# A hybrid decoder step on one core: the later adaLN columns made four pairs at a time

## The chip, the core and the metric

One Trainium2 chip, one of its NeuronCores. The metric is the time of one execution of the program on the device, in microseconds (us). The median of three runs of the kernel before is 998.04 us (995.92 to 1000.73).

## What is computed

One inference step of one decoder layer for 512 prompt tokens and 8 samples of 8 tokens (576 columns in all, width 1024). What matters here is the modulation, which every norm and every residual uses:

```python
cs = silu(c)                                   # 1 prompt row + 8 sample rows, width 1024
mod = cs @ ada_w + ada_b                       # (9, 6144)
sh1, sc1, g1, sh2, sc2, g2 = split(mod, 6)
h = rmsnorm(x, norm1_w) * (1 + sc1) + sh1
x = x + g1 * mixer(h)                          # in-projection, SSD | mLSTM | RG-LRU, out-projection
h = rmsnorm(x, norm2_w) * (1 + sc2) + sh2
x = x + g2 * (square(relu(h @ mlp_up)) @ mlp_down)
y = rmsnorm(x, final_norm_w)
```

`ada_w` has 1024 x 6144 weights of 4 bytes, 25 MB, for nine rows of `c`.

## The kernel before

Activations lie with the 1024 features on partitions, eight tiles (K tiles) of 128, and tokens along the free axis. A weight block of 128 output features is a tile `raw` of 128 x 1024, loaded by SP (line 128, three buffers), and split by ACT (`wh`, line 150) and DVE or GpSimd (`wl`, line 152) into two parts; `mm_k` (line 164) makes three products of it for each K tile and each half of the tokens, into an accumulator `g` of two PSUM banks. A block has 48 of these matmuls. In this text they are called block matmuls. There are 124 blocks: the in-projection, 16 of the out-projection, then the MLP.

Beside the blocks run generators: the SSD step of each head group and chunk (`ssd`), the mLSTM of each head (`mlstm`), the RG-LRU, the norms, and `ada_gen`. `unit` (line 179) calls `slot` in the middle and at the end of each block; a slot lets every active generator go on to its next `yield`. So a `yield` says after how many half blocks the next piece is written. The instructions are then put into queues by a list scheduler with a cost model of its own, which takes program order as priority and gives out tiles from pools: the final order on each engine is the scheduler's, and each engine works its queue off strictly in that order. SP's queue is also the order of nearly all loads.

Small products take PSUM tiles from the pool `psm` by `P()` (line 96): four tiles of one bank each, for all generators. In an SSD step `cb` and `xt` are two such tiles, `py` and `ps` two more: `cb` holds B C and B turned, `xt` the tokens of x turned (line 691); DVE makes `xdt` and `xend` from `xt` (line 698) and `att` from `cumb` (line 707), and TensorE makes `py` and `ps` from them (lines 729 to 734). In an mLSTM, `num` becomes `pt` by transposes (line 1063), and `pi` is C times q (line 1003).

The 6144 columns of `mod` are made in 24 pairs of 128 columns; pair q ends up in `modt[:, q]` (128 features x 2 x 9 rows). The first eight pairs (shift and scale of the first norm) are made at the start of the kernel and stay as they are. The pairs 8 to 23 are `ada_gen`'s, active from the second element of `ORDER` on. For each pair it loads two slabs of 128 x 1024 (line 238, 512 KB each, two buffers), waits `ADA_WAIT` = 3 slots, and then calls `ada_mm`: eight matmuls with `cs` of one K tile (32 columns, nine of them used) as weights and 256 columns of the slab as moving data. K tile k goes to column group k % 4 of the array, so that four K tiles run side by side and the bank `adap` holds four partial sums on its partitions 32j to 32j + 31. ACT copies the bank to `adarow` (line 220). A slot later `ada_sel` multiplies each half of `adarow` with the 0/1 matrix `sel` (line 228), which adds up the four partial sums and turns them onto partitions, and DVE adds the bias (line 229). After one more slot the next pair begins.

Of the kernel before, what the change touches and what calls it, by code (L numbers as in the profile page):

```python
# [22 lines left out]
FT = mybir.dt.float32  # L23
FR = mybir.dt.float32r
BF = mybir.dt.bfloat16
AF = mybir.ActivationFunctionType
OP = mybir.AluOpType
# [10 lines left out]
D, KT = 1024, 8  # L38
# [29 lines left out]
class Kernel:  # L68
# [162 lines left out]
                                op=OP.add)  # L231

    def ada_gen(self):
        for q in range(8, 24):
            t = []
            for c in range(2):
                t.append(self.rpool.tile([128, 1024], FT, name=self.name("ada"), tag="ada", bufs=2))
                self.nc.sync.dma_start(t[c], self.io["ada"][q, :, c * 1024:(c + 1) * 1024])
                if q == 8:
                    self.after(self.start_dma)  # L240
            for _ in range(ADA_WAIT):
                yield
            row = self.ada_mm(lambda k: t[k // 4][:, (k % 4) * 256:(k % 4 + 1) * 256])
            yield
            self.ada_sel(q, row)
            self.done.add(f"ada{q}")
            for _ in range(ADA_REST):
                yield

# [1212 lines left out]


N_TILES = 54
ADA_WAIT, ADA_REST = 3, 1
WARM = 14, 4, 4, 6
PAIR_AT = 3
W_AT = {0: 1, 2: 2, 4: 3}  # L1470
# [33 lines left out]
def _layout(a):  # L1504
    f = np.float32
    out = {}
    x = np.concatenate([a["x_prompt"].reshape(TP, D), a["x_sample"].reshape(TS, D)])
    out["x"] = x.T.reshape(KT, 128, NT).transpose(1, 0, 2)
    c = np.zeros((32, D), f)
# [3 lines left out]
    chunks = [v * 8 + k for pair in ((0, 1), (2, 3)) for k in range(8) for v in pair]  # L1513
    chunks += [4 * 8 + k for k in range(8)] + [5 * 8 + k for k in range(8)]
    w = a["ada_w"][0].reshape(KT, 128, 48, 128)[:, :, chunks]
    out["ada"] = w.reshape(KT, 128, 24, 2, 128).transpose(2, 1, 0, 3, 4).reshape(24, 128, 2048)
    ab = a["ada_b"][0].reshape(48, 128)[chunks].T

    w_in = a["w_in"][0]
# [1 line left out]
    z, xbc, dt, q, k, v, o, ig, fg, xr, gr = (w_in[:, pts[i]:pts[i + 1]] for i in range(11))  # L1521
# [50 lines left out]
    i = np.arange(128)  # L1572
# [3 lines left out]
    j = np.arange(64)  # L1576
# [5 lines left out]
    row = np.concatenate([np.arange(16), np.arange(32, 36), np.arange(64, 68)])  # L1582
# [56 lines left out]
```

## Time and profile before

| what | value |
|---|---|
| median of three runs (lowest, highest) | 998.04 us (995.92, 1000.73) |
| the profiled execution's own time | 995.4 us |
| its span, first to last instruction | 993.6 us |
| TensorE busy (share of the span) | 959.5 us (97%) |
| VectorE (DVE), ScalarE (ACT), GpSimd (POOL) busy | 590.2, 399.8, 203.8 us |
| mean granted clock of TensorE | 0.987 |
| moved by DMA | 119.62 MB, 120 GB/s |

The profile is of one execution. A row of the timeline has the start and the length in us, the engine, the line of the kernel, the operation, out<-in and a count; in brackets stands how long the engine was idle before and what ended that. PE is TensorE's matmuls, PEld its weight loads; a plain fp32 matmul leaves two records of each, one a pass. The ends of matmuls are modelled and overlap, so costs are read from starts. The time beyond the span, 1.8 us, is what lies around the program's instructions.

### The profile page before, as it was taken

The numbers are of one execution on the slowest core, as the hardware profiler recorded it, in microseconds if no ns is written. First come the engines' busy times: TensorE is split into PE (matmuls) and PEld (weight loads), VectorE is DVE, ScalarE is ACT, GpSimd is POOL, SyncE is SP. The second block draws the span as 40 slices with busy tenths as digits, with TensorE's granted clock in tenths as the row PEclk, the third lists the DMA queues.
The fourth block names the chain that finished last, engine by engine and source line by source line (L and its number), as shares of the span: only waits on it lengthen the run. The fifth ranks groups of instructions, "written<-read, shape, count | busy, mean of one in ns | idle before, by whom it ended". The sixth has DMA issues, their size and how long they took to land.

```text
span 993.6 us, 18146 instructions
## 1 busy us (share of the span) xinstructions
PE 959.5 (97%) x7369; PEld 904.1 (91%) x7370; DVE 590.2 (59%) x1180; ACT 399.8 (40%) x741; POOL 203.8 (21%) x220
## 2 busy tenths in 40 slices
PE   8999789889999999999999999999999999999996
PEld 5889778777788899999999999999999999999996
DVE  4669897887788377468444455533553355335544
ACT  3454744453646674345222234312441144114320
POOL 2836454532355532020000000000000000000032
PEclk8999999998999999999999999999999999999998
DMA  9721254654464333444222322222222222222202
GB/s 343 294 86 64 81 186 133 246 173 137 131 223 153 105 137 129 140 131 162 91 98 105 110 86 84 74 79 84 85 86 85 86 85 76 76 83 85 85 23 96
DMA packets 51220, 119.62 MB, mean 120 GB/s; under 512 B 6956, under 2 KB 17468, under 8 KB 51136
## 3 DMA queue, kind: packets, MB, share of 16 engines
q1 hardware_dynamic: 47024, 111.06, 32.7%
q10 hardware_dynamic: 3744, 6.85, 1.8%
q8 instruction: 58, 0.95, 0.4%
q0 software_dynamic: 368, 0.55, 0.2%
q14 instruction: 26, 0.21, 0.1%
HBM read 108.68 MB, written 9.76 MB: 119 GB/s over the span
## 4 chain that ended last, share of the span: by engine, by line
PE 76%; DVE 10%; ACT 4%; issue 3%; DMA 1%; POOL 0%; POOLq 0%; DVEq 0%; ACTq 0%
PE g L164 66%; DVE r L626 3%; PE adap L218 1%; PE g L1363 1%; DMA nmb<-scr_nm 1%; PE py L729 1%; PE lg L1129 1%; DVE att L707 1%; PE ps L734 1%; PE py L732 1%; DVE nmb L924 1%; DVE xbc L651 0%; DVE sp_e L494 0%; PE adas L228 0%; ACT r L620 0%
## 5 line engine op out<-in xcount | busy, mean ns | idle before, releaser
L150 ACT ACTIVATE wh<-raw 128x1024 fp32r<-128x1024 f32 x123 | 130.1, 1058 | 333.9 <-PE g L164 309.4
L164 PE MATMUL g<-hnh,wh 128*128 128x288 f32 x688 | 153.1, 302 | 10.1 <-ACT r L614 8.0
L164 PE MATMUL g<-hnh,wl 128*128 128x288 f32 x688 | 152.1, 299 | 0.6 <-DVE wl L152 0.6
L164 PE MATMUL g<-hnl,wh 128*128 128x288 f32 x688 | 151.8, 299 | 0.0
L152 DVE TENSOR_TENSOR wl<-raw,wh 128x1024 fp32r<-128x1024 f32 x97 | 118.7, 1225 | 29.5 <-ACT wh L150 29.4
L164 PEld LDWEIGHTS g<-hnh,wh 128*128 128x128 f32 x688 | 110.4, 189 | 19.3 <-ACT r L614 9.2
L164 PEld LDWEIGHTS g<-hnh,wl 128*128 128x128 f32 x688 | 111.6, 189 | 2.7 <-issue 1.2
L164 PEld LDWEIGHTS g<-hnl,wh 128*128 128x128 f32 x688 | 111.7, 189 | 0.8 <-issue 0.4
L164 PE MATMUL g<-h2h,wh 128*128 128x288 f32 (+1 forms) x512 | 110.9, 297 | 0.0
L164 PE MATMUL g<-h2l,wh 128*128 128x288 f32 (+1 forms) x512 | 110.9, 298 | 0.0
L164 PE MATMUL g<-h2h,wl 128*128 128x288 f32 (+1 forms) x512 | 110.0, 296 | 0.0
L307 DVE SCALAR_TENSOR_TENSOR xr<-g,modt,xr 128x288 f32<-128x288 f32 x38 | 19.7, 518 | 141.2 <-PE g L164 141.2
L164 PE MATMUL g<-hh,wl 128*128 128x288 f32 x480 | 102.9, 295 | 0.0
L164 PE MATMUL g<-hh,wh 128*128 128x288 f32 x480 | 102.5, 295 | 0.0
L164 PE MATMUL g<-hl,wh 128*128 128x288 f32 x480 | 102.4, 295 | 0.0
L1405 POOL TENSOR_SCALAR xr<-xr,vec 128x576 f32<-128x576 f32 (+2 forms) x8 | 15.2, 1900 | 383.8 <-ACT sqa L1237 363.4
L152 POOL TENSOR_TENSOR wl<-raw,wh 128x1024 fp32r<-128x1024 f32 x26 | 69.0, 2653 | 80.3 <-ACT wh L150 61.4
L164 PEld LDWEIGHTS g<-h2h,wl 128*128 128x128 f32 x512 | 83.4, 188 | 0.0
L164 PEld LDWEIGHTS g<-h2h,wh 128*128 128x128 f32 x512 | 83.1, 189 | 0.1
L164 PEld LDWEIGHTS g<-h2l,wh 128*128 128x128 f32 x512 | 83.0, 188 | 0.0
L164 PEld LDWEIGHTS g<-hh,wh 128*128 128x128 f32 x480 | 77.0, 188 | 0.0
L164 PEld LDWEIGHTS g<-hh,wl 128*128 128x128 f32 x480 | 77.0, 188 | 0.0
(399 smaller groups left out, 1652.7 us busy)
## 6 DMA issues: line engine op xcount, KB each, us to landing
raw<-w SPq DMA_DIRECT2D x124, 512.0 KB, 3.5
ada<-ada SPq DMA_DIRECT2D x32, 512.0 KB, 5.6
ada<-ada SPq DMA_DIRECT2D x32, 256.0 KB, 5.9
cumb<-scr_cum SPq DMA_DIRECT2D x16, 256.0 KB, 5.6
s<-s SPq DMA_DIRECT2D x16, 256.0 KB, 4.7
ssm_s<-s ACTq DMA_DIRECT2D x16, 256.0 KB, 2.9
x<-x SPq DMA_DIRECT2D x8, 288.0 KB, 4.7
xr<-x SPq DMA_DIRECT2D x8, 288.0 KB, 3.9
```

Source lines behind the costliest of these rows:

```text
L150: nc.scalar.activation(hi, raw, AF.Copy)
L152: eng.tensor_tensor(lo, raw, hi.bitcast(FT), op=OP.subtract)
L164: self.nc.tensor.matmul(pg.h[h][:m, :e], w(k), xx[:, h * HALF:h * HALF + e], start=start and n == 0, stop=stop and n == 2)
L218: nc.tensor.matmul(ps[32 * j:32 * j + 32, :256], self.cs[:, k, :], ks(k), start=k < 4, stop=k >= 4)
L307: self.nc.vector.scalar_tensor_tensor(dst[:, :HALF], pg.h[0][:, :HALF], gate[:, 0:1], x[:, :HALF], op0=OP.mult, op1=OP.add)
L626: nc.vector.scalar_tensor_tensor(a[:, :n], r[:, j:j + n], wcols[:, j:j + 1], a[:, :n], op0=OP.mult, op1=OP.add)
L707: self.eng("att").tensor_scalar(E[:, h * 128:(h + 1) * 128], cums[h2][:, h * 128:(h + 1) * 128], self.col1[:, c, hd:hd + 1], 0.0, op0=OP.a ...
L729: nc.tensor.matmul(o, xdt[:, h * 64:(h + 1) * 64], att[h // 4][:, hs], start=True, stop=not c)
L732: nc.tensor.matmul(o, S[:, h * 64:(h + 1) * 64], ce[h // 4][:, hs], start=False, stop=True)
L734: nc.tensor.matmul(pst, cb[:, 128:256], xend[:, :512], start=True, stop=True)
L924: self.eng("nmb").tensor_scalar(E[:, tk(c)], nmb[:, tk(c)], ecol(c), 0.0, op0=OP.add, op1=OP.min)
L1405: self.eng("fin").tensor_scalar(x, x, self.v("fnw")[:, o:o + 1], None, op0=OP.mult)
```

## The change

The 16 later pairs are made in four groups of four. The weights lie in DRAM in another order (`ada4`): slab i of a group holds K tile k of all four pairs, 4 x 256 columns. For each slab four matmuls run, all with the same weights `cs[:, k]`: pair j of the group goes to column group j, and its sum over all eight K tiles is made in PSUM. So `adap` is taken at the first slab of a group and given back after ACT's copy at the last. The partitions 32j to 32j + 31 of `adarow` then hold pair j's finished rows, and two full transposes per group (in place of eight selecting matmuls) turn them; DVE adds the bias of all four pairs in one instruction of 128 x 72. A slab is loaded one ahead, and `ADA_WAIT` is 2 slots for each slab, so a group takes 8 x 2 + 1 = 17 slots where four pairs took 4 x 5 = 20.

```diff
     def ada_gen(self):
-        for q in range(8, 24):
-            t = []
-            for c in range(2):
-                t.append(self.rpool.tile([128, 1024], FT, name=self.name("ada"), tag="ada", bufs=2))
-                self.nc.sync.dma_start(t[c], self.io["ada"][q, :, c * 1024:(c + 1) * 1024])
-                if q == 8:
-                    self.after(self.start_dma)
-            for _ in range(ADA_WAIT):
-                yield
-            row = self.ada_mm(lambda k: t[k // 4][:, (k % 4) * 256:(k % 4 + 1) * 256])
-            yield
-            self.ada_sel(q, row)
-            self.done.add(f"ada{q}")
-            for _ in range(ADA_REST):
-                yield
+        nc = self.nc
+        slabs = {}
+
+        def load(i):
+            if i < 32:
+                slabs[i] = self.rpool.tile([128, 1024], FT, name=self.name("ada"), tag="ada", bufs=2)
+                nc.sync.dma_start(slabs[i], self.io["ada4"][i])
+                if i == 0:
+                    self.after(self.start_dma)
+
+        load(0)
+        for i in range(32):
+            q, k = 8 + i // 8 * 4, i % 8
+            load(i + 1)
+            for _ in range(ADA_WAIT):
+                yield
+            if k == 0:
+                ps = self.P("adap")
+            t = slabs.pop(i)
+            for j in range(4):
+                nc.tensor.matmul(ps[32 * j:32 * j + 32, :256], self.cs[:, k, :], t[:, j * 256:(j + 1) * 256],
+                                 start=k == 0, stop=k == KT - 1)
+            if k < KT - 1:
+                continue
+            row = self.rpool.tile([128, 256], FT, name=self.name("adarow"), tag="adarow", bufs=2)
+            nc.scalar.activation(row, ps[:, :256], AF.Copy, scale=0.5)
+            yield
+            pt = self.P("adas")
+            for c in range(2):
+                nc.tensor.transpose(pt[:, c * 128:(c + 1) * 128], row[:, c * 128:(c + 1) * 128], self.ident)
+            src = pt[:, :256].rearrange("p (c j r) -> p j c r", c=2, j=4)[:, :, :, 0:9]
+            bias = self.v("adab")[:, 2 * q:2 * q + 8].rearrange("p (j c) -> p j c", j=4)
+            nc.vector.tensor_tensor(self.modt[:, q:q + 4], src, bias[:, :, :, None].to_broadcast([128, 4, 2, 9]),
+                                    op=OP.add)
+            for j in range(4):
+                self.done.add(f"ada{q + j}")
...
-ADA_WAIT, ADA_REST = 3, 1
+ADA_WAIT = 2
...
-    out["ada"] = w.reshape(KT, 128, 24, 2, 128).transpose(2, 1, 0, 3, 4).reshape(24, 128, 2048)
+    w = w.reshape(KT, 128, 24, 256)
+    out["ada"] = w[:, :, :8].transpose(2, 1, 0, 3).reshape(8, 128, 2048)
+    out["ada4"] = w[:, :, 8:].reshape(KT, 128, 4, 4 * 256).transpose(2, 0, 1, 3).reshape(32, 128, 1024)
```

In the new program the lines behind the change are 22 higher: line 691 is 713 there, 729 is 751, 1063 is 1085.

Since the scheduler sets the order, the change moves more than its own instructions. TensorE's queue during the in-projection, well behind the generators, before: a pair's eight matmuls (`adap`, two rows of four) stand together between the block matmuls (`g`).

```order
L164 MATMUL g_4678<-hnh_435,wl_4538 128x288 x2
L218 MATMUL adap_4709<-ada_4597,cs 32x256 x4
L218 MATMUL adap_4709<-ada_4599,cs 32x256 x4
L164 MATMUL g_4678<-hnh_475,wh_4537 128x288 x2
L164 MATMUL g_4678<-hnl_476,wh_4537 128x288 x2
```

The same stretch after the change:

```order
L164 MATMUL g_4505<-hnh_616,wl_4366 128x288 x2
L255 MATMUL adap_4494<-ada_4429,cs 32x256 x4
L164 MATMUL g_4580<-hnh_297,wh_4438 128x288 x2
L164 MATMUL g_4580<-hnl_298,wh_4438 128x288 x2
L164 MATMUL g_4580<-hnh_297,wl_4439 128x288 x2
```

A slab's four matmuls stand alone, and as often again between the blocks. In the whole order the later ada matmuls stand in 31 pieces where they stood in 17, and four slabs are cut in two by another instruction where one was.

TensorE's queue between the first two chunks of the SSD, before: the matmuls `py` and `ps` of one chunk, then at once `cb` and the four transposes `xt` of the next (the names with `xbc` are its inputs).

```order
L729 MATMUL py_1434<-att_1372,xdt_1368 64x128 x4
L729 MATMUL py_1434<-att_1379,xdt_1368 64x128 x4
L734 MATMUL ps_1435<-xend_1369,cbm_1365 128x512
L688 MATMUL cb_1486<-xbc_736,xbc_720 128x128
L689 MATMUL cb_1486<-vec,xbc_720 128x128
L691 MATMUL xt_1487<-vec,xbc_752 128x128
L691 MATMUL xt_1487<-vec,xbc_840 128x128
```

After, the rows from `py` to `cb`, and then, behind 23 block matmuls of which the last is shown, `xt` and the next ada slab:

```order
L751 MATMUL py_1432<-att_1368,xdt_1364 64x128 x4
L756 MATMUL ps_1433<-xend_1365,cbm_1361 128x512
L751 MATMUL py_1432<-att_1375,xdt_1364 64x128 x4
L710 MATMUL cb_1480<-xbc_736,xbc_720 128x128
L711 MATMUL cb_1480<-vec,xbc_720 128x128
L164 MATMUL g_1589<-hnh_616,wl_1326 128x288
```

```order
L164 MATMUL g_1715<-hnl_436,wh_1452 128x288 x2
L713 MATMUL xt_1481<-vec,xbc_752 128x128
L713 MATMUL xt_1481<-vec,xbc_840 128x128
L713 MATMUL xt_1481<-vec,xbc_918 128x128
L713 MATMUL xt_1481<-vec,xbc_1005 128x128
L164 MATMUL g_1715<-hnh_435,wl_1453 128x288 x2
L255 MATMUL adap_1267<-ada_1521,cs 32x256 x4
```

The block matmuls moved ahead of `xt`, and an ada slab came behind it. (The first piece ends with the first of the 23, the second begins with the last two.)

TensorE's queue at the first mLSTM's `pt`, before and after: where block matmuls led straight to `pt`, two slabs (one piece) now stand between.

```order
L164 MATMUL g_2665<-hnl_617,wh_2347 128x288 x2
L164 MATMUL g_2665<-hnh_616,wl_2348 128x288 x2
L1063 MATMUL pt_2566<-vec,num_2215 128x128 x3
L1063 MATMUL pt_2566<-vec,num_2216 128x128
L1064 MATMUL pt_432_2567<-vec,num_2216 128x64
```

```order
L164 MATMUL g_2657<-hnh_616,wl_2346 128x288 x2
L255 MATMUL adap_2447<-ada_2452,cs 32x256 x4
L255 MATMUL adap_2447<-ada_2618,cs 32x256 x4
L1085 MATMUL pt_2552<-vec,num_2207 128x128 x3
L1085 MATMUL pt_2552<-vec,num_2208 128x128
```

SP's queue at the first SSD step had its two `cumb` loads, then a pair's two slabs; now a slab's load stands between the two `cumb` loads.

## The prediction

> **What bounds the kernel now.** I read the page first, then the windows by stage, then TensorE's waits, then the timeline around single ada pieces. The page's head and its first engine:
>
> ```profile
> span 993.6 us, 18146 instructions
> ...
> PE 959.5 (97%) x7369; PEld 904.1 (91%) x7370; DVE 590.2 (59%) x1180; ACT 399.8 (40%) x741; POOL 203.8 (21%) x220
> ```
>
> TensorE sets the time; what is taken off its queue is worth its full length only where it does not wait. The windows (length, then busy us of PE, PEld, DVE, ACT, POOL; then clock, DMA share, GB/s) show where that is:
>
> ```profile
> 100.00:200.00 100.00, 88.47 (x706) 76.33 (x707) 85.14 (x178) 55.16 (x119) 49.65 (x45) 0.98 0.50 162
> 200.00:300.00 100.00, 92.90 (x764) 79.53 (x763) 77.31 (x209) 49.91 (x134) 38.81 (x31) 0.97 0.50 164
> 300.00:400.00 100.00, 99.31 (x756) 91.39 (x755) 68.40 (x133) 62.16 (x125) 39.18 (x38) 1.00 0.37 128
> 400.00:470.00 70.00, 70.00 (x578) 64.71 (x578) 45.28 (x93) 35.70 (x77) 5.70 (x9) 1.00 0.46 151
> ```
>
> From 100 to 300 us (stretch A) PE is idle for 11.5 + 7.1 = 18.6 us while DVE is 77 to 85% busy. From 300 us (stretch B) PE is full. TensorE's waits, first in 100 to 300 us, then in 300 to 500 us (us in total, times, longest):
>
> ```profile
> PE g L164 <- ACT r L614: 5.6, 2, 4.3
> PE pt L1063 <- DVE num L1059: 4.3, 1, 4.3
> PE py L729 <- DVE att L711: 2.8, 2, 1.5
> PE pu L829 <- DVE modt L229: 1.7, 1, 1.7
> ...
> PE pc L822 <- DVE modt L229: 0.3, 1, 0.3
> ```
>
> ```profile
> PE g L164 <- DVE ii L1165: 0.7, 1, 0.7
> ```
>
> So A waits for evacuations and for DVE's chains in the SSD and mLSTM steps, among them 1.7 + 0.3 = 2.0 us behind `modt`, an ada instruction; B waits 0.7 us in all. The later ada work is spread over both; the windows of its matmul line (PE busy with its records) say how:
>
> ```profile
> 119.00:300.00 181.00, 6.42 (x96) 2.50 (x96) 0.98 0.54 174
> 300.00:486.00 186.00, 11.32 (x160) 4.30 (x160) 1.00 0.40 134
> ```
>
> A pair leaves 16 records (8 matmuls, two passes each), so 6 pairs lie in A and 10 in B.
>
> **What one ada piece costs TensorE.** One pair between the matmuls of a block (start, length, what, count):
>
> ```profile
> 344.00 0.43 PE L164 MATMUL g<-hnl,wh 128*128 128x288 f32 x2
> 344.26 0.42 PE L164 MATMUL g<-hnh,wl 128*128 128x288 f32 x2
> 344.62 1.07 PE L218 MATMUL adap<-ada,cs 128*32 128x256 f32 x16
> 345.62 0.53 PE L164 MATMUL g<-hnh,wh 128*128 128x288 f32 x2
> 345.99 0.43 PE L164 MATMUL g<-hnl,wh 128*128 128x288 f32 x2
> ```
>
> Two block matmuls start every 0.265 us, 0.133 each. From 344.26 to 345.99 are 1.73 us and four of them (0.53): the pair costs 1.20. One record of it lasts 0.38 us:
>
> ```profile
> L218 PE MATMUL adap<-ada,cs x384: 379/379/636, 14.9 to 465.8; 128*32 128x256 f32 x192
> ```
>
> so the 16 begin over 1.07 - 0.38 = 0.69 us: four rounds of four column groups at once, 0.23 a round. The rest, 1.20 - 4 x 0.23 = 0.28, is paid for going in and out, once for each piece that stands alone in the queue.
>
> The Trainium skill, TensorEngine Tiling (Array Packing), section Tiling Modes, says that changing the tiling mode drains the array; the 0.28 agrees in kind, and it speaks against this change, which makes more pieces. The skill's TensorE: Matmul & The Clock Gate, section Part 2, gives about 128 cycles to a drain, by which (an estimate) a piece would pay 2 x 0.053 = 0.11 us, and the 14 more pieces counted below 1.5 us, not 3.9; the sum would be 2.4 us better. The row decides.
>
> The selecting matmuls of a pair, which go, and two full transposes inside a block, which come in their place:
>
> ```profile
> 340.05 0.42 PE L164 MATMUL g<-hnh,wh 128*128 128x288 f32 x2
> 340.31 0.51 PE L228 MATMUL adas<-vec,adarow 128*128 128x9 f32 x4
> 340.67 0.51 PE L164 MATMUL g<-hnl,wh 128*128 128x288 f32 x2
> 341.02 0.43 PE L164 MATMUL g<-hnh,wl 128*128 128x288 f32 x2
> ```
>
> ```profile
> 318.64 0.43 PE L164 MATMUL g<-hnh,wh 128*128 128x288 f32 x2
> 318.91 0.30 PE L164 MATMUL g<-hnl,wh 128*128 128x288 f32 x1
> 319.05 0.38 PE L1063 MATMUL pt<-vec,num 128*128 128x128 f32 x2
> 319.19 0.38 PE L164 MATMUL g<-hnl,wh 128*128 128x288 f32 x1
> 319.40 0.27 PE L1063 MATMUL pt<-vec,num 128*128 128x128 f32 x1
> ```
>
> A selection costs 341.02 - 340.05 - 0.53 = 0.44 us; two transposes cost 319.40 - 318.64 - 0.53 = 0.23 us.
>
> **The sum, part by part.** Pieces are counted in the order of the two programs. The transposes of the second group of four stand where B's first pair stood, so 16 slabs lie in A and 16 in B. A slab is four matmuls on four column groups, two rounds. Four slabs are cut in two by another instruction (one in A, three in B; before, one in B); the halves no longer run side by side, which adds two rounds, 0.46, beside the extra piece.
>
> - B before: 11 pieces x 0.28 + 40 rounds x 0.23 + 0.46 + 10 selections x 0.44 = 17.1 us. After: 18 x 0.28 + 32 x 0.23 + 3 x 0.46 + 3 pairs of transposes x 0.23 = 14.5. Gain 2.7 us, and nothing there hides it.
> - A before: 6 x 0.28 + 24 x 0.23 + 6 x 0.44 = 9.8. After: 13 x 0.28 + 32 x 0.23 + 0.46 + 0.23 = 11.7. Loss 1.85 us, but against 18.6 us of idle. It costs nothing where a piece stands ahead of a wait, as two slabs now do ahead of this one:
>
> ```profile
> 225.45 0.87 PE L1063 MATMUL pt<-vec,num 128*128 128x128 f32 x3 [4.26 <-DVE num L1059]
> ```
>
>   and 1.85 if every piece delays what DVE waits for. I take half, 0.9.
> - The 2.0 us behind `modt`: one such instruction is left in A where six were, and DVE stands less often before a selection. Between 0 and 2.0; I take 1.0.
> - ACT and DVE:
>
> ```profile
> L220 ACT ACTIVATE adarow<-adap 128x256 f32<-128x256 f32 x24 | 9.1, 379 | 16.9 <-PE adap L218 16.8
> L698 DVE TENSOR_TENSOR xdt<-xt,col 128x512 f32<-128x512 f32 x8 | 5.5, 684 | 0.6 <-PE xt L691 0.3
> L229 DVE TENSOR_TENSOR modt<-adas,vec 128x18 f32<-128x18 f32 x24 | 4.0, 169 | 16.0 <-PE adas L228 16.0
> ```
>
>   ACT loses 12 copies, 4.5 us. DVE loses 16 x 0.169 = 2.7 and gets four of 72 columns, each between 0.169 and the 0.684 of 512 columns; near the small end, 0.2. Both engines have room in B, so zero; in A it is part of the half above.
> - SP issues the same 32 loads of 512 KB, but from the third on each waits for the matmuls of the slab two before it, and loads stand behind it. The tightest place is the first SSD step: the second `cumb` load now stands behind the third slab's load, which waits for the first slab on PE. In the trace, SP, DVE and the landing times of `cumb` (us, min/median/max):
>
> ```profile
> 118.31 0.93 SPq L667 DMA_DIRECT2D cumb<-scr_cum x2
> 120.31 1.11 SPq L238 DMA_DIRECT2D ada<-ada  x2
> ```
>
> ```profile
> 127.25 3.33 DVE L707 TENSOR_SCALAR att<-cumb,col 128x128 f32<-128x128 f32 x8
> ```
>
> ```profile
> DMA to landing us min/median/max: 4.6/5.8/7.9
> ```
>
>   If it leaves at 120.3 it lands at 126.1, at the longest at 128.2; DVE needs this second tile for the fifth of the eight instructions, 127.25 + 4 x 0.42 = 128.9. Zero, then, covered by the conv work that DVE does first; without that cover it would cost the 1.6 us by which the load leaves later.
>
> Sum: -2.7 + 0.9 - 1.0 = -2.8, without the halves between -4.7 (both zero cost and full relief) and -0.8. The profiled run took 995.4 us (span 993.6 and 1.8 around it), 2.6 under the median of the three runs, 998.04, with a spread of 995.92 to 1000.73. So 992.6 for that run, and **995.2** against the median.
>
> The Trainium skill, TensorE: Matmul & The Clock Gate, section Part 4, puts one transpose (of bf16, in a kernel) at about 275 ns; by that (an estimate) four groups would cost 2.2 us, not 0.9, and the sum would be 1.3 worse. The rows here show two for 0.23.
>
> **Rivals.** A measurement of this kernel can tell about 0.5% (5.0 us) from no change: below 993.0 is faster, above 1003.0 slower.
>
> 1. *The holes swallow the ada work* (faster). The order puts three pieces straight ahead of places that wait: two slabs ahead of `pt` (1.20), one slab each shortly ahead of the first two `py` (0.28 + 0.46 = 0.74 each). If all three are hidden, A turns from +1.85 to -0.8; with all 2.0 us behind `modt` gone: -2.7 - 0.8 - 2.0 = -5.5, 992.5. For it: the waits of 4.3 and 2.8 us are DVE's, and DVE's work there hardly changes. Against: a later PE also feeds DVE later.
> 2. *A bank is missing* (slower). `adap` now keeps one of the four banks of its pool from the first slab to the eighth, through most of A and B. The order shows it: in one SSD step the `xt` transposes come 23 block matmuls after `cb` where they stood beside it (3.1 us), in another 19 where 4 stood (2.0 us), and the mLSTM's `pi` 21 later (2.8 us). DVE's `xdt` and all behind it wait for `xt`. If DVE's chain, 85% busy in 100 to 200 us, takes each delay in full: -0.8 + 7.9 = +7.1, 1005.1. It decides once the `py` that follows waits over about 2 us more than now. Against: the next `py` stand at the same block matmul as before, and DVE has other work queued.
> 3. *Given back* (no difference): A's 1.85 is paid in full and one of these delays (2.0) reaches PE: -0.8 + 2.0, 999.2.
>
> **How the numbers follow.** The forecast gets 0.48: B's gain is counted and unhidden, A's part lies between two bounds. Rival 1 gets 0.25, rival 3 0.14, rival 2 0.13. Hence faster 0.25, same 0.62, slower 0.13. The range leaves out rival 2 and the lowest twentieth of rival 1's side: from 992.5 less 2 us, the distance of the lowest run from the median, to 999.2 plus 2.3: 990.5 to 1001.5.
>
> **What would show it.** Right: PE still without waits in 300 to 470 us; the ada pieces there one slab long, about 0.74 us each; the block matmul that is at 486 us now some 3 us earlier relative to its place at 300 us; A as long as before within 2 us. Rival 1: the waits of `pt` and `py` shrink by what stands ahead of them. Rival 2: `py` or the matmuls behind `xt` wait longer, DVE shows idle time before `xdt`. Wrong altogether: a piece of one slab that costs over 1.0 us, or waits of PE in B for a load or a bank.

## The result and the profile after

The change makes the kernel slower: 1010.0 us (median of 16 runs, 1000.93 to 1017.13) against 996.13 us (16 runs, 992.72 to 1000.87) of the kernel before, run beside it; ratio 1.0117, interval [1.0094, 1.0140]. 995.2 was forecast, 1001.5 was the upper end of the range. (The ratios and the medians at equal clock below leave out executions more than 1.5% above the fastest of their kernel, three of these sixteen; the other thirteen have a median of 1009.07 us.) The profiled execution took 1012.96 us, its span is 1011.2 us.

The page's head and engines after. TensorE's busy time has risen by 9.5 us. By the counts of the prediction the change takes 0.8 us of work from TensorE; the rise goes with the clock, which stood at half for 41.0 us up to the end of stretch B (defined below) in place of 20.5; half of the difference, 10.2 us (an estimate), is work that took longer:

```profile
span 1011.2 us, 17993 instructions
...
PE 969.0 (96%) x7314; PEld 905.4 (90%) x7314; DVE 591.9 (59%) x1168; ACT 397.9 (39%) x729; POOL 199.6 (20%) x220
```

The windows by stage after (columns as before):

```profile
100.00:200.00 100.00, 86.97 (x699) 73.32 (x697) 82.27 (x169) 52.05 (x106) 41.94 (x42) 0.98 0.50 159
200.00:300.00 100.00, 89.70 (x712) 74.02 (x712) 75.78 (x193) 46.93 (x123) 41.25 (x32) 0.95 0.54 178
300.00:400.00 100.00, 95.77 (x689) 85.49 (x690) 64.69 (x135) 59.12 (x127) 34.29 (x35) 0.97 0.34 118
400.00:470.00 70.00, 70.00 (x549) 63.17 (x548) 42.26 (x86) 32.19 (x72) 12.27 (x16) 1.00 0.36 126
```

Two things differ. TensorE is idle for 23.3 us between 100 and 300 us (18.6 before), and for 4.2 us in the stretch from 300 to 400 us, which had been full (0.7). And the clock is 0.95 and 0.97 where it was 0.97 and 1.00.

TensorE's waits after, first in 100 to 300 us, then in 300 to 500 us:

```profile
PE g L164 <- ACT r L636: 7.4, 3, 4.3
PE adas L264 <- DVE C L1007: 2.8, 1, 2.8
PE py L751 <- DVE att L733: 2.1, 3, 1.3
PE pt L1086 <- DVE num L1081: 2.0, 1, 2.0
PE adap L255 <- DMA ada<-ada: 1.6, 1, 1.6
PE g L164 <- ACT v L924: 1.2, 1, 1.2
PE g L164 <- ACT q L924: 1.0, 1, 1.0
PE pk L942 <- DVE s L857: 1.0, 1, 1.0
```

```profile
PE g L164 <- DVE zz L881: 3.6, 2, 2.8
PE g L164 <- ACT ot L1095: 1.4, 1, 1.4
PE adap L255 <- DMA ada<-ada: 1.3, 1, 1.3
```

The waits that were to shrink did: `pt` from 4.3 to 2.0, `py` from 2.8 to 2.1, and those behind `modt` are gone. New ones came: the two transposes (`adas`) wait 2.8 us until DVE's `C` is done, which I read as a wait for the bank that `C` empties, and block matmuls are queued behind them; two slabs are waited for (1.6 and 1.3); block matmuls wait for `zz`, `ot`, `q`.

To place the loss in all kernels alike I count block matmuls, of which each profile has the same 5,856 records, and read their starts in the timeline. From where 480 of them lie behind to where 1200 do (113.7 to 308.3 us before; below, A) the kernel before needs 194.6 us, the changed one 207.7; from there to 2256 (485.7 us; B) 177.4 and 178.0. So 13.1 us go in A and 0.6 in B; 3.2 go ahead of A, where both orders are the same, and go with 10.2 us more at half clock; behind B, where the orders are the same again, it is 0.6.

The 13.1 us can be taken apart. TensorE's idle time in A rises from 13.6 to 19.5 us, 5.9 more. Its time at half clock in A, by the clock's records in the trace, rises from 6.8 to 17.1 us; half of the 10.3, or 5.1 us, is lost if TensorE had work all that time. The 1.85 us of work that the prediction counted make the rest: 5.9 + 5.1 + 1.85 = 12.9, an estimate.

The windows around two half-clock stretches after (length, PE busy and records, clock, DMA share, GB/s):

```profile
280.60:284.00 3.40, 1.81 (x11) 1.00 0.82 268
284.10:287.50 3.40, 3.40 (x14) 0.50 0.09 33
287.60:291.00 3.40, 3.40 (x27) 1.00 0.96 326
296.50:301.00 4.50, 2.21 (x18) 1.00 0.48 187
301.10:308.00 6.90, 6.03 (x25) 0.51 0.22 80
```

Each follows a stretch in which TensorE was about half idle; in the first, 14 records fit where 27 fit right after. So a wait can be paid twice, once for itself and again in clock. The Trainium skill, TensorE: Matmul & The Clock Gate, section Part 1, says that the gate halves the clock after an idle window of about 3.4 us, and that the windows run freely; the lengths of 3.4 and 6.8 us in the clock's records agree. The Trainium skill, TensorE: Matmul & The Clock Gate, section Why this matters for your kernels, advises against idle gaps over about 3 us. Here half clock followed a stretch of 3.40 us that was busy for 1.81, with no single wait in it over 1.22 us.

**The kept bank.** What forecast and order had named as rival 2 stands in the timeline. The view of the tile `xt` lists who waited for it (us, times); before, after, and in e13_bank_free below:

```profile
  DVE xdt L698: 0.3, 1
```

```profile
  DVE xdt L720: 6.0, 4
```

```profile
  DVE xdt L723: 1.2, 3
```

At the second chunk of the SSD, where the order had shown 23 block matmuls between `cb` and `xt`, the timeline after has, on TensorE and on DVE:

```profile
138.57 0.27 PE L711 MATMUL cb<-vec,xbc 128*128 128x128 f32 x1
141.74 0.60 PE L713 MATMUL xt<-vec,xbc 128*128 128x128 f32 x4
```

```profile
139.41 0.28 DVE L715 TENSOR_TENSOR cbm<-cb,vec 128x128 f32<-128x128 f32 x1
142.38 0.69 DVE L720 TENSOR_TENSOR xdt<-xt,col 128x512 f32<-128x512 f32 x1 [2.69 <-PE xt L713]
```

Before, `xt` started 0.11 us behind that `cb` (135.19 and 135.30) and DVE did not wait. But the 2.69 us are not what the chain lost. Before, DVE had other work first and came to this `xdt` only at 138.14, 5.32 us behind the start of the first chunk's `py` (132.82); after, it is 6.37 us (136.01 and 142.38). So 1.05 us are lost here.

The larger step comes one chunk later: the second `xdt` starts 4.2 us later than before, the third 9.0. The third chunk's `cb` and `xt` on TensorE before, then after:

```profile
144.02 0.27 PE L689 MATMUL cb<-vec,xbc 128*128 128x128 f32 x1
144.13 0.60 PE L691 MATMUL xt<-vec,xbc 128*128 128x128 f32 x4
```

```profile
148.58 0.27 PE L711 MATMUL cb<-vec,xbc 128*128 128x128 f32 x1
150.50 0.64 PE L255 MATMUL adap<-ada,cs 128*32 128x256 f32 x8 [1.64 <-DMA ada<-ada]
152.74 0.66 PE L713 MATMUL xt<-vec,xbc 128*128 128x128 f32 x4
```

After, a slab and then `py` matmuls stand between `cb` and `xt`, and the slab is waited for; with two buffers its load left SP at 143.24 us, behind the piece at 142.54 that frees the buffer. From the second `xdt` to the third it is 6.7 us before and 11.5 after; 7.0 with the bank given back (e13, e17), 10.4 with a third buffer (e3), but also 10.2 in e15, which keeps no bank. So the order at this place costs more than the wait for `xt`, and the kept bank is one way to get such an order, not the only one.

### The profile page after: what moved, and what is told of

It is laid out like the page before. It is cut to its first block, busy times and chain, and to the rows that moved or that the text cites. A ratio compares the mean times of both kernels' runs of the same rounds, so it can differ in the third digit from the quotient of the medians.

```text
span 1011.2 us, 17993 instructions
## 1 busy us (share of the span) xinstructions
PE 969.0 (96%) x7314; PEld 905.4 (90%) x7314; DVE 591.9 (59%) x1168; ACT 397.9 (39%) x729; POOL 199.6 (20%) x220
## 4 chain that ended last, share of the span: by engine, by line
PE 75%; DVE 10%; issue 3%; ACT 3%; DMA 2%; POOL 0%; POOLq 0%; ACTq 0%; DVEq 0%
PE g L164 66%; DVE r L648 2%; DMA ada<-ada 1%; PE adap L255 1%; PE g L1385 1%; DVE bst L826 1%; DVE att L729 1%; PE py L751 1%; PE py L754 1%; PE lg L1151 1%; DMA nmb<-scr_nm 1%; DVE att L733 1%; PE ps L756 1%; PE pn L993 0%; DVE sp_e L516 0%
## 5 line engine op out<-in xcount | busy, mean ns | idle before, releaser
L164 PE MATMUL g<-hnh,wh 128*128 128x288 f32 x688 | 157.9, 310 | 15.6 <-ACT r L636 9.7
L164 PE MATMUL g<-hnl,wh 128*128 128x288 f32 x688 | 154.7, 305 | 0.0
L164 PEld LDWEIGHTS g<-hnh,wh 128*128 128x128 f32 x688 | 114.4, 195 | 27.4 <-ACT r L636 11.1
L164 PEld LDWEIGHTS g<-hnl,wh 128*128 128x128 f32 x688 | 114.6, 194 | 2.8 <-issue 2.1
L164 PEld LDWEIGHTS g<-hnh,wl 128*128 128x128 f32 x688 | 113.9, 194 | 1.0 <-issue 0.6
L152 POOL TENSOR_TENSOR wl<-raw,wh 128x1024 fp32r<-128x1024 f32 x26 | 65.3, 2511 | 87.3 <-ACT wh L150 84.7
```

The costliest lines, as they stand in the source:

```text
L152: eng.tensor_tensor(lo, raw, hi.bitcast(FT), op=OP.subtract)
L164: self.nc.tensor.matmul(pg.h[h][:m, :e], w(k), xx[:, h * HALF:h * HALF + e], start=start and n == 0, stop=stop and n == 2)
```

## The experiments

Theories: the **kept bank** (the bank of `adap` held over a group displaces `xt` and others); **pieces and loads** (31 small pieces, slabs that come just in time); a **disturbed order** (the list scheduler's order of before is a good one, and any other between 100 and 300 us costs).

One table holds what was measured. A and B are the stretches above in the profiled execution; "xdt" is DVE's wait for `xt`; "clock" the median granted clock of a kernel's runs. A and B hold what the clock did in that one execution: e10_tail_only has the order of before up to 300 us, and its A is 3.0 us longer with 6.8 us more of half clock. Nor do they hold the same ada work everywhere. A has the matmuls of six pairs (96 records) in the kernel before, e1, e4, e5, e10 and e18, of seven in e8 and e15, none in e7, and of eight in all others; in e2 the kept bank alone brings two pairs forward out of B. The last column needs a word. The 114 runs of the kernel before in these comparisons scatter with the clock, 0.74 us more for each 0.001 less. With that slope every run is brought to a clock of 0.986 (the median of before, whose time there is 997.6 us); the column is the median so obtained, less 997.6. The same code under another name gives +0.4, and the medians (5 to 13 runs each) are good to about 0.3 to 1.0 us. The kernel before itself lies between -0.6 and +0.5 in the five batches in which the kernels were run. I worked the column out after seeing the runs, and the verdicts on the texts on record use the ratio. The column also takes out a lower clock that a kernel's own waits may have caused, so it can be too kind: e8 has +6.0 there and 1.14% by the ratio.

| kernel | ratio [95%] | A | B | xdt | clock | at equal clock |
|---|---|---|---|---|---|---|
| before | 1 | 194.6 | 177.4 | 0.3 | 0.986 | 0 |
| after | 1.0117 [1.0094, 1.0140] | 207.7 | 178.0 | 6.0 | 0.985 | +9.3 |
| e1_same | 0.9985 [0.9959, 1.0011] | 194.3 | 178.2 | 0.3 | 0.990 | +0.4 |
| e2_hold | 1.0078 [1.0049, 1.0106] | 206.6 | 176.9 | 3.6 | 0.986 | +7.3 |
| e3_bufs3 | 1.0050 [1.0020, 1.0080] | 196.5 | 177.6 | 5.6 | 0.985 | +4.6 |
| e4_hybrid | 1.0030 [1.0004, 1.0057] | 194.4 | 179.5 | 0.3 | 0.986 | +2.3 |
| e5_null | 1.0059 [1.0035, 1.0083] | 199.0 | 180.3 | 0.5 | 0.986 | +4.8 |
| e6_two | 1.0075 [1.0047, 1.0104] | 201.2 | 177.7 | 3.8 | 0.981 | +2.9 |
| e7_late | 1.0118 [1.0088, 1.0147] | 194.1 | 188.2 | 0.6 | 0.982 | +7.6 |
| e8_pieces | 1.0114 [1.0081, 1.0147] | 200.1 | 178.9 | 0.6 | 0.980 | +6.0 |
| e9_cadence | 1.0030 [0.9998, 1.0062] | 202.8 | 173.7 | 0.6 | 0.986 | +4.5 |
| e10_tail_only | 0.9988 [0.9967, 1.0009] | 197.6 | 175.4 | 0.3 | 0.985 | -2.0 |
| e11_null_hold | 1.0130 [1.0092, 1.0168] | 205.6 | 181.8 | 2.4 | 0.982 | +10.0 |
| e12_pieces_hold | 1.0119 [1.0086, 1.0152] | 200.5 | 184.1 | 3.7 | 0.986 | +11.7 |
| e13_bank_free | 1.0016 [0.9991, 1.0041] | 194.9 | 176.9 | 1.2 | 0.989 | +4.2 |
| e14_free_bufs3 | 1.0013 [0.9989, 1.0037] | 197.1 | 176.8 | 1.2 | 0.989 | +3.4 |
| e15_null22 | 1.0100 [1.0071, 1.0130] | 204.6 | 176.8 | 0 | 0.981 | +6.4 |
| e16_hold22 | 1.0114 [1.0079, 1.0149] | 205.3 | 177.7 | 0.6 | 0.983 | +6.9 |
| e17_first_free | 1.0056 [1.0030, 1.0081] | 199.3 | 178.1 | 3.7 | 0.985 | +5.3 |
| e18_best | 1.0068 [1.0043, 1.0094] | 194.9 | 181.9 | 0.8 | 0.980 | +2.4 |

**e1_same**: the kernel before, unchanged.

> The kernel before, unchanged, as a measure of what two equal programs differ by, and for a second profile of it. Every theory: ratio 1.000 within 0.003. If the clock's half-speed stretches in the first 70 us are a matter of chance, this profile shows others there than the first one did (3.4 us at 25 and none near 62).

It shows the scatter of one code: 0.15% in the ratio, most of it clock.

**e2_hold**: the kernel before with the bank of `adap` kept over four pairs; nothing else.

```diff
-            row = self.ada_mm(lambda k: ...)
+            if q % 4 == 0:
+                keep = self.P("adap")
+            row = self.ada_mm(lambda k: ..., keep)
```

> The kernel before, its pairs and loads as they were, but the bank of adap is kept over four pairs instead of one. Bank theory (the kept bank makes the SSD and mLSTM steps wait, and the waits let the clock fall): slower by 6 to 12 us, with more than 10 us at half clock between 60 and 320 us, against 10 before and 24 after. Load theory (one slab at a time, just in time, stops TensorE and SP): no change, within 2 us. Piece theory (31 pieces in place of 17): no change, within 2 us.

12.0 us are lost in A, `xt` of the second chunk stands 19 block matmuls behind `cb`, and DVE waits 3.6 us for it. By the ratio it is 7.8 us, as the bank theory had it. The kept bank, with the order that the scheduler makes of it, is enough for two thirds of the change's loss.

**e3_bufs3**: the changed kernel, three slab buffers, two slabs loaded ahead.

```diff
-tag="ada", bufs=2)
+tag="ada", bufs=3)
...
-            load(i + 1)
+            load(i + 2)
```

> The changed kernel with three slab buffers and two slabs loaded ahead. Load theory: the 3.0 us of waits for slabs go, with what hangs on them: 4 to 8 us faster than the changed kernel, within 8 us of the kernel before. Bank theory and piece theory: the waits for slabs go, but it stays slower than before by 9 to 13 us.

About half of the loss goes, as the load theory had it, though the bank is kept and DVE still waits 5.6 us for `xt`. So late slabs are a part of it, and a wait of DVE is not always paid by TensorE.

**e4_hybrid**: pairs 8 to 15 as before, 16 to 23 in two groups with the changed code, so that A's order is untouched.

```diff
-        for q in range(8, 24):
+        for q in range(8, 16):          # as before
...
+        for i in range(16):             # groups 16-19, 20-23, the changed code
```

> Pairs 8 to 15 as before, pairs 16 to 23 in two groups of four as after, so that the mixing stage up to 300 us has the old order and only the stretch without waits has groups. Bank theory, and every theory that puts the loss into the mixing stage: within 3 us of the kernel before, between 3 us faster (the gain counted for the full stretch, 2.7, for eight of its ten pairs) and no change. Load theory: slower by 2 to 5 us, for the slabs come just in time there too. Piece theory: slower by 2 to 4 us.

A is as before (194.4), B is 2.1 us longer instead of shorter, with 2.5 us of idle time where there were 0.7: one-slab pieces, loaded one ahead, bring nothing even there. The bank theory's forecast (no slower) is missed, those of loads and pieces are met.

**e5_null**: the kernel before with `ADA_WAIT, ADA_REST = 4, 0` in place of 3, 1: the same instructions a slot later.

> The kernel before with the same five slots for a pair, but its matmuls one slot later (4 and 0 in place of 3 and 1): no bank is kept, nothing is added, only the scheduler's order changes. Bank theory: within 3 us of the kernel before. Chance theory (any other order of the mixing stage costs what the change cost): slower by 5 to 12 us.

0.6% slower, 4.4 us in A and 2.9 in B. A shift that changes no work costs half of what the change costs, as the chance theory had it and the bank theory had not.

**e6_two**: the changed kernel with two slabs in each piece (19 pieces), four slab buffers, `N_TILES` 53.

```diff
-            load(i + 1)
-            for _ in range(ADA_WAIT):
-                yield
+            if k % 2 == 0:
+                load(i + 2)
+                load(i + 3)
+                for _ in range(2 * ADA_WAIT):
+                    yield
```

> The changed kernel with four slab buffers and two slabs to a piece (19 pieces in place of 31), one tile fewer in the big pool to make room. The bank is kept as in the change. Piece theory: 4 us faster than the changed kernel for 12 fewer pieces and no more, so +0.7%. Load theory: no wait for slabs, at or below the kernel before, since the gain counted for the stretch without waits (5 us with these pieces) is then paid out. Bank theory: slower than before by 5 to 10 us.

By the ratio 7.5 us slower than before, which both the piece theory (0.7%) and the bank theory (5 to 10 us) had; the load theory is missed. At equal clock it is +2.9 where the changed kernel has +9.3; the ratio shows less of it, since its runs had a clock of 0.981.

**e7_late**: e3_bufs3 with `ADA_AT` 12 and `ADA_WAIT` 1, which moves the ada work from A to B.

> The changed kernel with three slab buffers, its ada work begun late (at element 12 of the order list in place of 1) and with one slot to a slab, so that nearly all of the mixing stage runs with four banks and without ada work. Bank theory: the mixing stage up to 300 us is shorter than before by up to 10 us, the PE time of six pairs; the ada work comes back behind it, at 0.77 us a slab alone and with waits for slabs; in all within 6 us of before on either side. Load theory: slower by 5 to 10 us, since a slab a slot leaves loads just in time.

Slower than either theory had it, 1.0118. A is as long as before with six pairs less in it, B 10.8 us longer. Of the 9.8 us that the prediction counted for ada work in A nearly nothing is won: idle time rises by 4.7 us and time at half clock by 6.8, and B pays for the work.

**e8_pieces**: the kernel before, each pair's eight matmuls in two pieces a slot apart (25 pieces), `ADA_WAIT, ADA_REST = 2, 1`.

```diff
+                if k == 3:
+                    yield
```

> The kernel before with each pair's eight matmuls in two pieces a slot apart (25 pieces in place of 17), so the bank is kept for one slot only. Piece theory: slower by 4 to 8 us. Bank theory: slower by 2 to 3 us, 8 more pieces at 0.28 us.

Slower than either theory had it by the ratio (1.14%): 5.5 us are lost in A and 1.5 in B, without a kept bank. Eight more pieces are worth 8 x 0.28 = 2.2 us by the forecast's price; the rest is order and clock (6.8 us more at half clock in A).

**e9_cadence**: all later pairs in groups, but two slabs together and eight matmuls a piece as before (20 pieces); bank kept.

```diff
+            for c in range(2):
+                for j in range(4):
+                    nc.tensor.matmul(ps[32 * j:32 * j + 32, :256], self.cs[:, 2 * m + c, :], ...)
```

> All sixteen later pairs in groups of four, as in the changed kernel, but with the pieces and the loads of the kernel before: two slabs are loaded together three slots ahead, and their eight matmuls are one piece, so 20 pieces instead of 31; the bank of `adap` is still kept over a group of four. Counted on TensorE it saves 16 selections of 0.44 us for four pairs of transposes of 0.23 us, about 6 us. Theory of the kept bank: as slow as the kernel before with the bank kept, 1.005 to 1.01, with some 10 us lost between 100 and 300 us. Theory of pieces and loads (the loss came from many small pieces and from slabs loaded late): 0.994 to 1.000. Theory of a disturbed order (any other order in 100 to 300 us costs, whatever makes it): 1.002 to 1.008, with half-clock stretches there above the 10 us of before.

The ratio lies in the range of the disturbed order, and outside those of the kept bank and of the pieces; but half clock in A fell (3.4 us for 6.8), which no theory had. B is 3.7 us shorter and A 8.2 longer. By the prediction's prices B should be 6.8 shorter (8 pieces, 32 rounds, 3 pairs of transposes: 10.3 us for 17.1); 3.0 us more of idle time there (3.7 for 0.7) are the difference.

**e10_tail_only**: pairs 8 to 15 as before, 16 to 23 in groups with e9's loop; nothing moves ahead of 300 us.

> Pairs 8 to 15 as before, pairs 16 to 23 in two groups of four with the pieces and loads of the kernel before (two slabs together, one piece), so that nothing moves before about 300 us and after it only the selections go: 8 of 0.44 us for two pairs of transposes of 0.23 us, 3.1 us less on TensorE where it does not wait. All theories that put the loss between 100 and 300 us: 0.995 to 0.998 and no new wait after 300 us. Theory of the kept bank as a cost of its own wherever it is kept: 1.000 to 1.005, with new waits after 300 us.

B is 2.0 us shorter, and -2.0 us is what stands at equal clock, of 3.1 counted; one new wait (`g` for DVE's `la`, 2.4 us) stands against it. The only changed version below the kernel before; by its ratio, which lies between the two forecasts, it cannot be told from it.

**e11_null_hold** and **e12_pieces_hold**: e5 and e8 with e2's kept bank.

> The kernel before with its slots shifted (four before a pair, none behind it) and in addition the bank of `adap` kept over four pairs; its partner is the shifted kernel without the kept bank, 1.0059. Theory of the kept bank: 5 to 12 us over the partner, 1.011 to 1.018, with block transposes that wait for a bank. Theory of a disturbed order (the bank only reshuffles): no systematic difference, anywhere from 1.000 to 1.010.

> The kernel before with every pair in two pieces, and in addition the bank of `adap` kept over four pairs; its partner is the same without the kept bank, 1.0114. Theory of the kept bank: 5 to 12 us over the partner, 1.016 to 1.024. Theory of a disturbed order: no systematic difference, from 1.003 to 1.015.

By the ratios the first pair differs by 0.7%, as the bank theory has it, the second by 0.05%, as it has not. At equal clock they differ by 5.2 and 5.7 us; for the second pair that rests on the correction, since the partner's clock was 0.980.

**e13_bank_free**: the changed kernel, but the bank is given back every second slab; 12 DVE additions of 0.42 us come in.

```diff
-            if k == 0:
+            if k % 2 == 0:
                 ps = self.P("adap")
...
-                                 start=k == 0, stop=k == KT - 1)
+                                 start=k % 2 == 0, stop=k % 2 == 1)
+            if k == 1:
+                row = ...                                   # ACT's copy, scale 0.5
+            elif k % 2 == 1:
+                nc.vector.scalar_tensor_tensor(row, ps[:, :256], 0.5, row, op0=OP.mult, op1=OP.add)
```

> The changed kernel with its slabs, loads and slots, but `adap` gives its bank back after every second slab: ACT copies the first two slabs' sum to `adarow`, DVE adds the other three to it (12 more DVE instructions of 128x256, by the rows of the profile between 0.17 and 0.68 us each, less than the changed kernel saved there). In its order `xt` of the second SSD step stands beside `cb` again, where the kept bank had put it 23 block matmuls later. Theory of the kept bank: the loss between 100 and 300 us shrinks from 13 us to 4 or less, 1.001 to 1.005 against the kernel before. Theory of small pieces and late loads: unchanged, 1.009 to 1.014. Theory of a disturbed order: in between, like any other order, 1.004 to 1.011.

1.0016 where the changed kernel has 1.0117, as the theory of the kept bank had it. A falls from 207.7 to 194.9 us, and `xt` stands beside `cb` again. Part of this is clock: A has no half clock here where the changed kernel's has 17.1 us, of which half, some 8.5 us, is lost time. Its windows:

```profile
100.00:200.00 100.00, 90.72 (x707) 75.27 (x707) 83.80 (x176) 52.82 (x113) 46.94 (x45) 0.98 0.53 169
200.00:300.00 100.00, 93.63 (x770) 78.82 (x774) 75.68 (x213) 52.51 (x139) 39.18 (x35) 1.00 0.52 164
```

15.7 us of idle time between 100 and 300 us where the changed kernel has 23.3, and no half clock between 200 and 300 us. At equal clock it is still 4.2 us behind the kernel before; a higher clock hides that in the ratio.

**e14_free_bufs3**: the same with three slab buffers, as in e3.

> The same with a third slab buffer, two slabs loaded ahead. Loads are a cost of their own: below the kernel with two buffers by some 3 to 7 us, as the third buffer made it with the bank kept (1.012 to 1.005). Kept bank as the main cost: 0.997 to 1.002, the best of the kernels with one-slab pieces. Loads cost nothing by themselves: same as with two buffers.

No difference from e13 that could be measured: once the bank is free, earlier loads bring no more.

**e15_null22** and **e16_hold22**: the kernel before with `ADA_WAIT, ADA_REST = 2, 2`, without and with the kept bank.

> The kernel before with two slots ahead of a pair and two behind it: same work, another order, bank not kept, `xt` of the second SSD step beside `cb`. Theory of a disturbed order (the order of before is a good one among many): 1.003 to 1.010. Theory that only the bank and pieces cost: 0.998 to 1.002.

> The same order rule with the bank of `adap` kept over four pairs; `xt` of the second SSD step now stands 19 block matmuls behind `cb`. Kept bank: 5 to 12 us over its partner with the bank free. Disturbed order alone: within 4 us of it, either way.

The order alone costs 1.0%, nearly as much as the change. On top of it the kept bank costs nothing that can be told (0.5 us at equal clock), although `xt` stands 19 block matmuls late: here, as in e9, where it is 19 too, DVE waits 0.6 us for it. The bank theory's 5 to 12 us are missed.

**e17_first_free**: the bank given back early in the first group alone.

> The changed kernel with the bank of `adap` given back every second slab in the first group of four alone, and kept in the other three. In its order `xt` of the second SSD step stands beside `cb`; the later `xt` stands 19 block matmuls behind `cb`, as in the changed kernel. If the first place is the cause: 1.001 to 1.005, and the 5.5 us that the changed kernel loses by 130 us are gone. If the second place is: 1.008 to 1.013, with the loss after 225 us. If each has its half: 1.005 to 1.008.

By the ratio in between, as if each place had its half; A is 199.3 us, 8.4 less than with the bank kept, and the 5.5 us lost by the 576th block matmul are gone. Of the 8.4 some 6.9 are clock in that execution (3.4 us at half for 17.1). At equal clock the first place gives 4.0 of the 5.1 us that freeing all four groups gives, though DVE still waits 3.7 us for the later `xt`.

**e18_best**: e9_cadence with the bank given back after each pair.

> All sixteen later pairs in groups of four, with the pieces and loads of the kernel before (two slabs together, eight matmuls in one piece) and with the bank given back after every pair (ACT copies the first pair's sum, DVE adds the other three). Counted on TensorE: 16 selections of 0.44 us go, four pairs of transposes of 0.23 us come, 6 us less, some 3.8 of them after 300 us, where TensorE does not wait. If the kept bank and the pieces were all that was wrong with the change: 0.994 to 0.997. If waits between 100 and 300 us fill up again: 0.997 to 1.001. If any other order costs: 1.002 to 1.010.

1.0068: both forecasts of a gain or of no change are missed, and the range of a disturbed order is met. A is as long as before (194.9), B 4.5 longer, with new waits for a slab (1.6 us), for DVE's addition to `adarow` (1.3), for `num` (1.2) and 6.8 us of half clock. By counted work it should be the best of all.

**The seven pairs with and without the kept bank**: what the bank costs at equal clock (us) and by the ratios, and DVE's wait for `xt` (without, with):

| order | at equal clock | by the ratios | xdt |
|---|---|---|---|
| before, e2 | 7.3 | 0.78% | 0.3, 3.6 |
| e5, e11 | 5.2 | 0.71% | 0.5, 2.4 |
| e8, e12 | 5.7 | 0.05% | 0.6, 3.7 |
| e13, after | 5.1 | 1.01% | 1.2, 6.0 |
| e14, e3 | 1.2 | 0.37% | 1.2, 5.6 |
| e18, e9 | 2.1 | -0.38% | 0.8, 0.6 |
| e15, e16 | 0.5 | 0.14% | 0, 0.6 |

Where the kept bank makes DVE wait for `xt`, it costs 5 to 7 us at equal clock in four pairs and 1.2 in the fifth, which has three slab buffers; where it doesn't, 0.5 to 2. The ratios, which leave the clock in, show a cost of 0.7 to 1.0% in three pairs and at most 0.4% in the others. So a kept bank often costs, by an amount that hangs on the order and the loads. That it does so through DVE's wait for `xt` is not shown: the pair with three slab buffers speaks against it, and so does the timeline above, where 2.69 us of that wait came to 1.05.

## Why the prediction was wrong

- **What it had right.** The price of a one-slab piece: after,

```profile
381.89 0.43 PE L164 MATMUL g<-hnh,wl 128*128 128x288 f32 x2
382.25 0.64 PE L255 MATMUL adap<-ada,cs 128*32 128x256 f32 x8
382.82 0.53 PE L164 MATMUL g<-hnh,wh 128*128 128x288 f32 x2
383.19 0.42 PE L164 MATMUL g<-hnl,wh 128*128 128x288 f32 x2
```

  383.19 - 381.89 - 0.53 = 0.77 us, where 0.74 was forecast. `pt` waits 2.3 us less, the 2.0 us behind `modt` are gone, and DVE's eight `att` of the first chunk take 3.31 us with no wait among them (3.33 before), so the moved `cumb` load does no harm. But the zero for the loads held for `cumb` alone: the slabs themselves come late, by 1.6 us in A and 1.3 in B, and a third buffer takes 4.7 us off at equal clock.
- **"Gain 2.7 us, and nothing there hides it" (B) failed.** The work left B, but B got waits of 3.7 us where it had 0.7 (the list above without the longest `zz`, which lies ahead of B, and 0.2 for `pt`), so it is 0.6 longer. With pieces and loads as before (e9, e10) B does get shorter, by 3.7 and 2.0, and there too new waits take a part of what was counted (6.8 and 3.1). The prediction had named this sign itself (waits of PE in B for a load).
- **"A's part lies between two bounds" failed, and this is the main step.** A's 18.6 us of idle time were taken for room: a loss of 1.85 at most. But A's idle time is made of waits between TensorE and the engines that feed it (ACT's `r`, DVE's `att`, `num`, `C` in the lists), and another order moves them: idle time rose by 5.9 us instead of taking work in, and A lost 13.1. At equal clock all sixteen kernels that changed A's order, the changed kernel among them, are 2.4 to 11.7 us behind the kernel before, the two that add no work (e5, e15) 4.8 and 6.4; of the two that left A's order alone one is ahead. (In e7 and e18 it is B that is longer, not A.) The bounds had no row behind them that spoke of the order.
- **Rival 2 named the right cause for about half of the loss, with low odds and too simple a price.** It was given 0.13, and "DVE has other work queued" stood against it. After the change DVE had none left at that place and stood for 2.69 us; before, it did have such work, so that `xdt` is only 1.05 us late, not the 3.1 of the displaced matmuls. One of its signs came (DVE idle before `xdt`), the other did not: the `py` that follows, which had waited 1.27 us, waited for nothing, since slabs and block matmuls stood ahead of it. The chain fell back at the third chunk, behind a late slab. Freeing the bank takes 5.1 us of the change's 9.3 at equal clock.
- **The clock was left out.** The thirteen counted runs of the changed kernel had 0.975 to 0.990, the median of before is 0.986; in the profile some 5.1 of A's 13.1 us are clock.

What stays open: why the 4.2 us of e13 remain, and the 4.8 and 6.4 of e5 and e15, which add no work. No one wait holds them: e5 has a new one of 3.9 us (`pu` for DVE's `bst`), e15 two of 3.1 and 2.9 (`adap` for `C`, `g` for `zz`), and both have more half clock in A (13.7 and 17.1 us for 6.8). That the third slab buffer (4.7 us) and the free bank (5.1) each take half of the loss and both together no more than 5.9 suggests that they cover for each other, not which wait they share.

## What to carry to other kernels

Where a list scheduler sets the order and TensorE waits in a chain with another engine, count a change's work, but price its order too: shift the kernel by a slot without changing its work and see what that costs, before a gain of a few us is believed. A PSUM bank that is kept longer can be a cost of its own in a pool of four (0.5 to 7 us here): look in the order for the tile that now comes late. An engine that stands waiting for that tile in the trace shows the place, not the price; for the price compare when the same step of the chain starts in both traces. Apply such a change where TensorE does not wait and leave the rest of the order alone, as in e10; even there no more than 2.0 us could be had, and e4, with one-slab pieces, lost 2.3.

## What the runs showed of the hardware

- Half clock came, between 70 and 900 us, in stretches of 3.4 us or twice that. In the changed kernel's profile four of five follow 3.4 us in which TensorE was busy for 38 to 53%; the fifth (106.6 us) follows 3.4 us without a matmul. In the other profiles the share goes from 0 to 89% (e3, at 197.0 us), so the share of one such stretch alone does not tell. In that range the profiles have from 3.4 us (e13) to 25.4 us (e11) of it. Ahead of A the same code had 13.7 us of it in one execution (before) and 3.4 in another (e1).
- One program's runs differ by it: thirteen runs of the changed kernel range from 1000.93 us at a mean clock of 0.990 to 1015.26 at 0.975; in the kernel before it is 0.74 us for each 0.001. Comparing at equal clock cut the scatter of its 114 runs from 3.1 to 1.2 us (standard deviation).
- Two full fp32 transposes inside a stream of block matmuls cost little: in e10,

```profile
409.43 0.43 PE L164 MATMUL g<-hnh,wl 128*128 128x288 f32 x2
409.70 0.38 PE L274 MATMUL adas<-vec,adarow 128*128 128x128 f32 x2
409.84 0.51 PE L164 MATMUL g<-hnh,wh 128*128 128x288 f32 x2
410.19 0.43 PE L164 MATMUL g<-hnl,wh 128*128 128x288 f32 x2
```

  410.19 - 409.43 - 0.53 = 0.23 us, as forecast.
